# Every second low part of the down weights by an adding transfer instead of a VectorE subtraction

## The chip, the cores and the metric

The kernel runs on one core of a Trainium2 chip. The metric is the time of one execution on the device in microseconds (us). TensorE (PE) multiplies matrices, VectorE (DVE), ScalarE (ACT) and GpSimd (POOL) work elementwise, and SyncE (SP) issues transfers, which run on 16 DMA engines. Here POOL has so far had only small jobs.

## The reference, cut to what matters

One encoder layer over 256 tokens of width 2048: a SwiGLU feed-forward layer of width 5632, attention, a second such feed-forward layer, and a gated embedding, each between two RMS norms. The part that the change touches is the product with `w_down` of both feed-forward layers.

```python
def _swiglu(u, w_gate, w_up, w_down):
    return (jax.nn.silu(u @ w_gate) * (u @ w_up)) @ w_down

for i in range(DEPTH):
    f = _swiglu(_rmsnorm(h, ffn1_pre_g[i]), ffn1_w_gate[i], ffn1_w_up[i], ffn1_w_down[i])
    h = h + 0.5 * _rmsnorm(f, ffn1_post_g[i])
    m = _mixer(_rmsnorm(h, mix_pre_g[i]), w_qkv[i], na_rpb[i], out_g[i], w_o[i])
    h = h + _rmsnorm(m, mix_post_g[i])
    f = _swiglu(_rmsnorm(h, ffn2_pre_g[i]), ffn2_w_gate[i], ffn2_w_up[i], ffn2_w_down[i])
    h = h + 0.5 * _rmsnorm(f, ffn2_post_g[i])
```

All inputs are float32.

## The kernel before, in words

**Split products.** A float32 value does not fit TensorE's fast format fp32r, so each operand is split into a high part, rounded to fp32r, and a low part, the rest. A product is then three matmuls: high by high, low by high, high by low (lines 114, 115, 116). The activations' split lies ready in SBUF (`xh`, `xl`); the weights are split as they arrive.

**load_pairs** (line 62) does that. A transfer on SP's queue (line 69) brings four blocks of 128 weight rows by 512 columns, 1 MB, into a tile `raw`, of which there are three. Blocks are split in pairs: ScalarE writes the high parts of two blocks into a tile `wh`, VectorE the low parts into a tile `wl`; there are seven of each. Where the rows carry a gain `g` (gate, up, q, k, v and others) lines 79 and 80 do it block by block. Where they carry none, line 74 copies 128 x 1024 elements with rounding, and line 75 subtracts: `wl = raw - wh`. Only the down weights and the small `w_ple_proj` come without a gain.

**product** (line 89) walks through the rows of a product in steps of up to eight blocks. For each step it calls `load_pairs`, then multiplies: for the first 128 tokens all eight blocks, three matmuls each, then for the second 128 tokens the same eight blocks again. A step of eight is 48 matmuls, two `raw` tiles (here called A and B) and four pairs, P0 and P1 from A, P2 and P3 from B.

**The order of the work.** A scheduler keeps each engine's instructions close to the program's order; an engine executes its own in order and waits at semaphores for the others. `wh` and `wl` tiles are taken in turn, so pair number n waits until PE has read pair n - 7 for the second tokens. That means that P0, P1 and P2 of a step can be split a whole step ahead, while P3 waits for P0 of the step just before it: PE reads that for the last time early in the second half of that step. A `raw` tile comes free for SP's next load when its last reader is done.

**swiglu** (line 220) works in three groups of 4, 4 and 3 column blocks of 512 (`FF_GROUPS`): gate and up for each block of the group, then the down product of the group's 16, 16 or 12 row blocks into each of four column blocks of the output (line 276). 16 rows are two steps of eight; 12 rows are a step of four and one of eight. A group of 16 rows has so 8 steps of eight in a row, and there are four such groups in the kernel (two per layer): 32 steps. The two groups of 12 rows add 8 steps of eight, each between steps of four.

Of the kernel before, what the change touches and what calls it, by code (L numbers as in the profile page):

```python
# [10 lines left out]
AF = mybir.ActivationFunctionType  # L11
ALU = mybir.AluOpType
# [21 lines left out]
def encoder_layer(ctx: ExitStack, tc: tile.TileContext, a: dict, out: bass.AP):  # L34
# [6 lines left out]
    nc = tc.nc  # L41
# [19 lines left out]
    def load_pairs(w, r0, nk, c0, g):  # L61


        pairs = []
        for k0 in range(0, nk, 4):
            n = min(4, nk - k0)
            raw = wpool.tile([P, 4, NB], F32, name="raw", bufs=3)
            rows_ = w[r0 + k0 * P : r0 + (k0 + n) * P, c0 : c0 + NB]
            raw_loads.append(nc.sync.dma_start(raw[:, :n], rows_.rearrange("(k p) n -> p k n", p=P)))
            for j in range(0, n, 2):  # L70
                wh = wpool.tile([P, 2, NB], F32R, name="wh", bufs=7)
                wl = wpool.tile([P, 2, NB], F32R, name="wl", bufs=7)
                if g is None:
                    nc.scalar.copy(wh, raw[:, j : j + 2])  # L74
                    nc.vector.tensor_tensor(wl, raw[:, j : j + 2], wh.bitcast(F32), op=ALU.subtract)  # L75
                else:
                    for i in range(min(2, n - j)):
                        k = r0 // P + k0 + j + i
                        nc.scalar.activation(wh[:, i], raw[:, j + i], AF.Copy, scale=g[:, k : k + 1])  # L79
                        nc.vector.scalar_tensor_tensor(  # L80
                            wl[:, i], raw[:, j + i], g[:, k : k + 1], wh[:, i].bitcast(F32),
                            op0=ALU.mult, op1=ALU.subtract,
                        )
                pairs.append((wh, wl))
        return pairs
# [3 lines left out]
    def product(  # L89
# [11 lines left out]
        for n in steps or [nk % SUPER] * (nk % SUPER > 0) + [SUPER] * (nk // SUPER):  # L101
            if ahead is not None:
                ahead(s0)
            pairs = load_pairs(w, r0 + s0 * P, n, c0, g)
            for t in range(NT):
                tok = slice(t * P, (t + 1) * P)
                for k in range(n):
                    if mid is not None and t == NT - 1 and s0 + n == nk and k == n - MID:
                        mid()
                    wh, wl = pairs[k // 2]  # L110
                    xh, xl = lhs[s0 + k]
                    lead = first and s0 + k == 0
                    tail = last and s0 + k == nk - 1
                    nc.tensor.matmul(acc[t], xh[:, tok], wh[:, k % 2], start=lead, stop=False)  # L114
                    nc.tensor.matmul(acc[t], xl[:, tok], wh[:, k % 2], start=False, stop=False)  # L115
                    nc.tensor.matmul(acc[t], xh[:, tok], wl[:, k % 2], start=False, stop=tail)  # L116
            s0 += n
            if jobs:
                for job in later:
                    job()  # L120
                later.clear()
# [173 lines left out]
    with ExitStack() as att:  # L295
# [18 lines left out]
        for t in range(NT):  # L314
            for h0 in range(0, n_h, 2):
                raw = attn.tile([P, 2, S], F32, name="na_raw", tag="pr", bufs=2)
# [292 lines left out]
```

## Time and profile before

| | |
|---|---|
| median of the runs | 1991.86 us (1991.73 to 1991.98) |
| the profiled execution's own time | 1990.87 us |
| its span in the trace | 1988.8 us |
| PE busy | 1969.9 us |
| DVE, ACT busy | 1155.9 us, 1050.2 us |
| POOL busy | 25.4 us, 47 instructions |
| moved by DMA | 377.02 MB, mean 190 GB/s |

The profile is of one execution. A row of its groups names the line, the engine, the operation and the tiles; then stand the count, the busy time in us, the mean of one in ns, and the idle time of that engine just before, with what ended it. A matmul's duration (389 ns) is longer than the distance between two of them, since they are pipelined: distances are read from start to start.

### The profile page before, as it was taken

Reading aid. Unit: us, or ns where it says so; the run is one execution under the profiler, and the core shown is the slowest. Engines: PE = TensorE matmul, PEld = TensorE weight load, DVE = VectorE, ACT = ScalarE, POOL = GpSimd, SP = SyncE. Lnnn points to the kernel's source line nnn. Section 1 sums busy time; section 2 is a strip of 40 time slices with the busy share of each in tenths; the row PEclk is TensorE's granted clock in tenths of the full one; section 3 lists DMA queues with packets and bytes.
Section 4 is the critical chain, followed back from the end, with each engine's and each line's share of the span. In section 5 each row is a group of like instructions: output and inputs, shape, how many; then the busy total and the mean of one; then the engine's idle time right before and its main releaser. Section 6 shows DMA issues by size and latency. Waiting matters only on the chain.

```text
span 1988.8 us, 23482 instructions
## 1 busy us (share of the span) xinstructions
PE 1969.9 (99%) x8936; PEld 1629.7 (82%) x8936; DVE 1155.9 (58%) x1659; ACT 1050.2 (53%) x1613; POOL 25.4 (1%) x47
## 2 busy tenths in 40 slices
PE   8999999999999999999999999999999999999998
PEld 7888888888888877888888888888888888888886
DVE  5755455655465666566565575654465545565764
ACT  7645455544455455655556564544454534454663
POOL 0000000000000000000000000000000000000000
PEclk9999999999999999999999999999999999999999
DMA  8755555555555557364554555555555555555562
GB/s 302 242 192 187 194 193 189 190 191 188 194 198 183 197 183 224 134 201 138 170 170 168 187 192 200 179 203 175 206 181 200 179 201 184 197 183 203 172 213 102
DMA packets 194561, 377.02 MB, mean 190 GB/s; under 512 B 10768, under 2 KB 13968, under 8 KB 194192
## 3 DMA queue, kind: packets, MB, share of 16 engines
q1 hardware_dynamic: 194448, 375.52, 55.1%
q8 instruction: 70, 1.15, 0.2%
q14 instruction: 43, 0.35, 0.0%
HBM read 373.40 MB, written 2.10 MB: 189 GB/s over the span
## 4 chain that ended last, share of the span: by engine, by line
PE 96%; DMA 1%; DVE 1%; ACT 1%; issue 0%; POOL 0%; SPq 0%; DVEq 0%; POOLq 0%; ACTq 0%
PE down L116 8%; PE down L114 8%; PE down L115 8%; PE up L116 8%; PE up L114 8%; PE up L115 8%; PE gate L116 8%; PE gate L115 8%; PE gate L114 8%; PE tr L150 2%; PE q L116 1%; PE q L115 1%; PE q L114 1%; PE pg L116 1%; PE pg L114 1%; PE k L116 1%
## 5 line engine op out<-in xcount | busy, mean ns | idle before, releaser
L79 ACT ACTIVATE wh<-raw,row_g 128x512 fp32r<-128x512 f32 x1024 | 686.7, 717 | 456.0 <-PE up L115 184.2
L80 DVE SCALAR_TENSOR_TENSOR wl<-raw,row_g,wh 128x512 fp32r<-128x512 f32 x1024 | 708.6, 749 | 335.9 <-ACT wh L79 335.8
L75 DVE TENSOR_TENSOR wl<-raw,wh 128x1024 fp32r<-128x1024 f32 x180 | 220.0, 1224 | 167.5 <-ACT wh L74 153.1
L74 ACT CAST wh<-raw 128x1024 fp32r<-128x1024 f32 x180 | 189.8, 1055 | 213.1 <-PE down L115 168.7
L114 PE MATMUL gate<-wh,u_h 128*128 128x512 f32 x704 | 276.5, 393 | 6.0 <-ACT wh L79 6.0
L116 PE MATMUL gate<-wl,u_h 128*128 128x512 f32 x704 | 275.2, 391 | 0.0
L115 PE MATMUL gate<-wh,u_l 128*128 128x512 f32 x704 | 275.1, 391 | 0.0
L114 PE MATMUL down<-wh,hid_h 128*128 128x512 f32 x704 | 274.5, 390 | 0.0
L116 PE MATMUL down<-wl,hid_h 128*128 128x512 f32 x704 | 274.1, 389 | 0.0
L116 PE MATMUL up<-wl,u_h 128*128 128x512 f32 x704 | 274.0, 389 | 0.1
L114 PE MATMUL up<-wh,u_h 128*128 128x512 f32 x704 | 274.0, 389 | 0.0
L115 PE MATMUL down<-wh,hid_l 128*128 128x512 f32 x704 | 273.9, 389 | 0.0
L115 PE MATMUL up<-wh,u_l 128*128 128x512 f32 x704 | 273.9, 389 | 0.0
L114 PEld LDWEIGHTS gate<-wh,u_h 128*128 128x128 f32 x704 | 132.9, 189 | 32.9 <-ACT wh L79 6.0
L116 PEld LDWEIGHTS gate<-wl,u_h 128*128 128x128 f32 x704 | 132.7, 188 | 27.9 <-DVE wl L80 0.3
L116 PEld LDWEIGHTS up<-wl,u_h 128*128 128x128 f32 x704 | 132.1, 188 | 28.2 <-DVE wl L80 0.5
L115 PEld LDWEIGHTS gate<-wh,u_l 128*128 128x128 f32 x704 | 132.8, 189 | 27.0
L114 PEld LDWEIGHTS up<-wh,u_h 128*128 128x128 f32 x704 | 132.1, 188 | 27.5 <-ACT wh L79 0.3
L115 PEld LDWEIGHTS up<-wh,u_l 128*128 128x128 f32 x704 | 132.1, 188 | 27.4
L115 PEld LDWEIGHTS down<-wh,hid_l 128*128 128x128 f32 x704 | 132.2, 188 | 27.4
L116 PEld LDWEIGHTS down<-wl,hid_h 128*128 128x128 f32 x704 | 132.1, 188 | 27.4
L114 PEld LDWEIGHTS down<-wh,hid_h 128*128 128x128 f32 x704 | 132.2, 188 | 27.0
(122 smaller groups left out, 1813.6 us busy)
## 6 DMA issues: line engine op xcount, KB each, us to landing
raw<-in_ffn_w_up SPq DMA_DIRECT2D x88, 1024.0 KB, 5.1
raw<-in_ffn_w_down SPq DMA_DIRECT2D x88, 1024.0 KB, 5.0
raw<-in_ffn_w_gate SPq DMA_DIRECT2D x84, 1024.0 KB, 5.1
raw<-in_w_qkv SPq DMA_DIRECT2D x48, 1024.0 KB, 5.1
raw<-in_w_o SPq DMA_DIRECT2D x16, 1024.0 KB, 5.0
raw<-in_w_ple_gate SPq DMA_DIRECT2D x16, 1024.0 KB, 5.0
raw<-in_ffn_w_gate SPq DMA_DIRECT2D x7, 512.0 KB, 4.4
xb<-in_xT SPq DMA_DIRECT2D x8, 256.0 KB, 3.2
```

The lines of the kernel that those rows point to most:

```text
L74: nc.scalar.copy(wh, raw[:, j : j + 2])
L75: nc.vector.tensor_tensor(wl, raw[:, j : j + 2], wh.bitcast(F32), op=ALU.subtract)
L79: nc.scalar.activation(wh[:, i], raw[:, j + i], AF.Copy, scale=g[:, k : k + 1])
L80: nc.vector.scalar_tensor_tensor(wl[:, i], raw[:, j + i], g[:, k : k + 1], wh[:, i].bitcast(F32), op0=ALU.mult, op1=ALU.subtract,)
L114: nc.tensor.matmul(acc[t], xh[:, tok], wh[:, k % 2], start=lead, stop=False)
L115: nc.tensor.matmul(acc[t], xl[:, tok], wh[:, k % 2], start=False, stop=False)
L116: nc.tensor.matmul(acc[t], xh[:, tok], wl[:, k % 2], start=False, stop=tail)
L150: nc.tensor.transpose(tr[:, k], x[:, k * P : (k + 1) * P], ident)
```

## The change

In a step of more than four blocks without a gain, the second pair of each `raw` tile (`j` = 2: P1 and P3) no longer goes through VectorE. ScalarE writes `wh` as before, then writes the negative of the rounded weight into `wl` (line 76 of the changed kernel), and a transfer on GpSimd's queue adds the raw weights to it in SBUF (line 77): `wl = -high + raw`. The first pair of each tile (`j` = 0), steps of four, and `w_ple_proj` are made as before. Lines behind the edit move down by 5, so line 74 of before is 79, 75 is 80, 116 is 121.

```diff
             for j in range(0, n, 2):
                 wh = wpool.tile([P, 2, NB], F32R, name="wh", bufs=7)
                 wl = wpool.tile([P, 2, NB], F32R, name="wl", bufs=7)
-                if g is None:
+                if g is None and j and nk > 4:
+
+                    nc.scalar.copy(wh, raw[:, j : j + 2])
+                    nc.scalar.activation(wl, raw[:, j : j + 2], AF.Copy, scale=-1.0)
+                    nc.gpsimd.dma_start(wl, raw[:, j : j + 2], accum_op=ALU.add)
+                elif g is None:
                     nc.scalar.copy(wh, raw[:, j : j + 2])
                     nc.vector.tensor_tensor(wl, raw[:, j : j + 2], wh.bitcast(F32), op=ALU.subtract)
```

How the instructions stand on ScalarE in the first feed-forward layer, first group, second column block (`down_1667` before and `down_1671` after are its accumulator for the first tokens, the number plus one that for the second). Before:

```order
L264 COPY f<-down_1514 128x512
L74 CAST wh<-raw 128x1024 x4
L264 COPY f<-down_1667 128x512
L74 CAST wh<-raw 128x1024 x4
L264 COPY f<-down_1668 128x512
```

With the change:

```order
L269 COPY f<-down_1514 128x512
L79 CAST wh<-raw 128x1024
L75 CAST wh<-raw 128x1024
L76 ACTIVATE wl<-raw 128x1024
L79 CAST wh<-raw 128x1024
L75 CAST wh<-raw 128x1024
L76 ACTIVATE wl<-raw 128x1024
L79 CAST wh<-raw 128x1024
L269 COPY f<-down_1671 128x512
L75 CAST wh<-raw 128x1024
L76 ACTIVATE wl<-raw 128x1024
L79 CAST wh<-raw 128x1024
```

Each step has gone from four to six conversions on ScalarE; the two new ones stand right behind the high parts of P1 and P3.

GpSimd between the factors of the first feed-forward layer's input norm and those of its output norm, before:

```order
L138 TENSOR_SCALAR m<-m 128x1
L139 TENSOR_TENSOR r<-m,mhalf 128x1
L138 TENSOR_SCALAR m<-m 128x1
L139 TENSOR_TENSOR r<-m,mhalf 128x1
```

With the change:

```order
L143 TENSOR_SCALAR m<-m 128x1
L144 TENSOR_TENSOR r<-m,mhalf 128x1
L77 DMA wl<-raw 128x1024 x40
L143 TENSOR_SCALAR m<-m 128x1
L144 TENSOR_TENSOR r<-m,mhalf 128x1
```

All 40 transfers of a layer stand alone on that queue; nothing else is between them. The second layer has 40 more.

TensorE in the first step of that column block, first tokens, from the second matmul of the third block on (`DMASW` is the semaphore of a transfer issued by GpSimd):

```order
L120 MATMUL down_1671<-wh,hid_l 128x512
L121 MATMUL down_1671<-wl,hid_h 128x512 [waits DMASW4_49]
L119 MATMUL down_1671<-wh,hid_h 128x512
L120 MATMUL down_1671<-wh,hid_l 128x512
L121 MATMUL down_1671<-wl,hid_h 128x512
```

TensorE's order is the same as before, but the third matmul of the third block (P1) and of the seventh (P3) now wait for the adding transfer in place of VectorE.

SP's loads of the down weights wait for it too, since it reads `raw`. Before:

```order
L69 DMA raw<-in_ffn_w_down 128x4x512 [waits DMAHW0_49,DVE_49]
```

With the change:

```order
L69 DMA raw<-in_ffn_w_down 128x4x512 [waits DMASW0_49,DMAHW3_49,DVE_49,Activation_49]
```

The place is a load into a `raw` tile whose last reader was VectorE and now is the adding transfer.

## The prediction

> **What bounds the kernel now.** I read the page first: engines, granted clock, chain, queues.
>
> ```profile
> PE 1969.9 (99%) x8936; PEld 1629.7 (82%) x8936; DVE 1155.9 (58%) x1659; ACT 1050.2 (53%) x1613; POOL 25.4 (1%) x47
> PE   8999999999999999999999999999999999999998
> PEclk9999999999999999999999999999999999999999
> PE 96%; DMA 1%; DVE 1%; ACT 1%; issue 0%; POOL 0%; SPq 0%; DVEq 0%; POOLq 0%; ACTq 0%
> q1 hardware_dynamic: 194448, 375.52, 55.1%
> ```
>
> TensorE is busy for 1969.9 of 1988.8 us at a full granted clock, and 96% of the chain of waits is TensorE. The change leaves its matmuls alone, so at most the 19 us in which it idles could be won, and its slices show those at the start and the end, where no down weight is split. What counts is whether TensorE begins to wait. The last row gives the resource that the change draws on: weight loads fill 55.1% of the 16 DMA engines.
>
> Next the down stage itself, by windows: two steps of eight (208.26 to 230.02 us), and about one step of four and one of eight in the 12-row group.
>
> ```profile
> core 0: us, PE busy (x) PEld busy (x) DVE busy (x) ACT busy (x) POOL busy (x), PEclk, DMA share, GB/s
> 208.26:230.02 21.76, 21.76 (x97) 18.02 (x96) 9.80 (x9) 9.51 (x10) 0.00 (x0) 1.00 0.55 193
> 675.20:691.50 16.30, 16.30 (x78) 13.58 (x77) 11.02 (x12) 8.29 (x12) 0.00 (x0) 1.00 0.50 171
> ```
>
> TensorE fills the window. VectorE and ScalarE work for less than half of the two steps. DMA is busy for 0.55 x 21.76 = 12.0 us, 6.0 us per step of 10.88 us; a step has two loads, so one load of 1 MB takes all engines for 3.0 us.
>
> **What comes off and on the compute engines.**
>
> ```profile
> L79 ACT ACTIVATE wh<-raw,row_g 128x512 fp32r<-128x512 f32 x1024 | 686.7, 717 | 456.0 <-PE up L115 184.2
> L75 DVE TENSOR_TENSOR wl<-raw,wh 128x1024 fp32r<-128x1024 f32 x180 | 220.0, 1224 | 167.5 <-ACT wh L74 153.1
> L74 ACT CAST wh<-raw 128x1024 fp32r<-128x1024 f32 x180 | 189.8, 1055 | 213.1 <-PE down L115 168.7
> L116 PE MATMUL down<-wl,hid_h 128*128 128x512 f32 x704 | 274.1, 389 | 0.0
> ```
>
> Each of the 40 steps of eight loses two subtractions: 80 x 1.224 = 98 us off VectorE. It is off the chain: the subtractions themselves wait for ScalarE, and the matmuls that read them show 0.0 us of idle time ahead. Worth: 0. ScalarE gets 80 negating copies. The trace has none; the nearest row is line 74, the same tile shape and types, 1.055 us, so 84 us. Its bounds are line 79's 0.717 us for half the size with a scale, and twice that, 1.43 us: 57 to 115 us. They fit: 9.51 + 4 x 1.055 = 13.7 of 21.76 us per two steps. Without that cover they would cost 84 us. GpSimd gets 80 issues, with 25.4 us of work in the whole kernel; nothing of it stands between them, so what they cost there is latency, counted next.
>
> **The time that P3's transfer has.** P1 and the other pairs can be made a step ahead; P3 waits for a buffer that comes free in the step before. Timeline rows, the first three TensorE, then ScalarE and VectorE:
>
> ```profile
> 214.84 0.39 PE L115 MATMUL down<-wh,hid_l 128*128 128x512 f32 x1
> 219.14 0.39 PE L116 MATMUL down<-wl,hid_h 128*128 128x512 f32 x1
> 223.90 0.39 PE L116 MATMUL down<-wl,hid_h 128*128 128x512 f32 x1
> ...
> 215.26 1.05 ACT L74 CAST wh<-raw 128x1024 fp32r<-128x1024 f32 x1 [5.27 <-PE down L115]
> 216.62 1.06 ACT L74 CAST wh<-raw 128x1024 fp32r<-128x1024 f32 x1 [0.30 <-PE down L115]
> ...
> 216.35 5.30 DVE L75 TENSOR_TENSOR wl<-raw,wh 128x1024 fp32r<-128x1024 f32 x4 [5.57 <-ACT wh L74]
> ```
>
> At 214.84 PE reads the high part of P0's second block for the last time, and ScalarE starts on P3 of the next step at 215.26. A step ends with the matmul at 219.14; from there to 223.90 are 21 matmuls, 0.227 us each, 48 of them 10.88 us. The one at 223.90 is the seventh block's third, the first to read P3's `wl`. VectorE has it ready at about 217.6, 6.3 us early. Now ScalarE writes high part and negative by 215.26 + 2 x 1.055 = 217.4, and the transfer has 223.9 - 217.4 = **6.5 us** from issue to landing. Each us above is a stall of TensorE in each of 32 steps. P1's negative is the fifth conversion of that round, ready at 215.26 + 5 x 1.055 and short waits, about 221, and first read in the third block of the step after next, 219.37 + 10.88 + 8 x 0.227 = 232.1: 11 us. In the 12-row groups P3 takes P2's buffer, free some 2.9 us later, and a step of four, 5.44 us, lies between: 9 us.
>
> Behind a late transfer SP waits too: `raw` comes free only when it has landed, and SP's queue is in order.
>
> ```profile
> SPq L69 <- DVE wl L75: 442.1, 92, 8.8
> raw<-in_ffn_w_down SPq DMA_DIRECT2D x88, 1024.0 KB, 5.0
> raw<-in_ffn_w_gate SPq DMA_DIRECT2D x7, 512.0 KB, 4.4
> raw<-in_w_ple_proj SPq DMA_DIRECT2D x4, 512.0 KB, 3.8
> ```
>
> SP waits up to 8.8 us for that reader as it is, 442.1 / 92 = 4.8 us on average, then loads for 5.0 us. So the loads have slack, and one may come some us later without ScalarE going short.
>
> **What one adding transfer costs.** No transfer within SBUF and none on GpSimd's queue is in this trace, so I bound it by loads. A load of 512 KB lands after 3.8 to 4.4 us, one of 1 MB after 5.0, of which 3.0 are moving; about 2.0 are fixed. Low end: 512 KB pass once, 1.5 us of all engines, landing in 3.8. Middle: the engines must fetch the old `wl` as well as `raw`, so 1 MB is read: 3.0 us, landing in 5.0 alone. High end: four passes (two reads, the sum, the write) one after the other, 6.0 us. I take the middle, since adding cannot be done without the second read, and writing can run beside reading, as it does in the loads.
>
> The Trainium skill says the same of reduction by DMA on the page "Collectives: The Full Stack", section "The bandwidth ceiling: the fold count and why AG ≠ RS ≠ AR": the add itself is not what makes it slower, the two source reads are, and they halve the rate. Its page "DMA: Bandwidth & Descriptors", section "Anatomy of one DMA — SWDGE (gpsimd) path", gives 2.0 us plus bytes / 436e3 for a transfer from GpSimd, an estimate of 3.2 us for 512 KB; by that P3 would have 3.3 us to spare and the change would cost nothing. No row here shows either.
>
> **The sum.** Demand on the DMA engines per step of eight: 6.0 + 2 x 3.0 = 12.0 us in a step of 10.88 us. So they become the bound: 1.1 us per step. The other view is latency: 5.0 us alone; when a load is in flight beside it all the time, sharing the engines by half, 3.0 more, 8.0 us, a stall of 1.5. With the engines full, the second is nearer. I take 1.3 us: 32 x 1.3 = **42 us**. The 12-row groups: three loads, 9.0, plus 6.0 is 15.0 in 16.3 us, 0. ScalarE, VectorE, GpSimd: 0. Against the profiled execution: 1990.9 + 42 = 2033; the median is 1 us above that, so **2034 us**, 2.1% slower. Its own range is 0.6 to 2.1 us per step, 2011 to 2059.
>
> **Rivals.**
>
> *Hidden.* The second read costs the engines little, or SBUF answers faster than the memory the loads read. With up to 2.4 us a transfer the demand is 10.8 us, and landing stays below 6.5. For it: 3.8 us for a plain 512 KB leave 2.7 us of room. Against it: there is nearly no reserve, with two users on the same engines. Time: 1992, not slower.
>
> *Slow adding.* The passes are not overlapped. Three of them, 4.5 us per transfer: 6.0 + 9.0 = 15.0 per step, 4.1 over, 132 us; in the 12-row groups 9.0 + 9.0 = 18.0 in 16.3, 8 x 1.7 = 14 us: 2138. Four: 7.1 x 32 + 4.7 x 8 = 265 us, 2257. Nothing in this profile speaks for or against.
>
> *GpSimd is slow to issue.* If writing out the transfer takes 4 us more than SP's 2.0 fixed, it lands after 9.0 alone, and P3 stalls TensorE for 2.5 us while the engines still have idle time: 32 x 2.5 = 80 us, 2072. The row that bears on it is thin:
>
> ```profile
> L425 POOL TENSOR_TENSOR ro<-sso,mhalf 128x4 f32<-128x4 f32 x8 | 8.5, 1059 | 304.4 <-DVE sso L423 304.4
> L69 SPq DMA_DIRECT2D raw<-in_ffn_w_down x88: 367/368/368, 162.2 to 1844.7; - x88
> ```
>
> GpSimd takes 1.06 us for four elements per partition, where SP issues a whole load in 0.37.
>
> *It brings something.* VectorE's 98 us would have to stand on the chain; TensorE's waits on it there sum to nothing in the page's groups. 1985 would be a third of TensorE's 19 idle us.
>
> **Chances.** Forecast 0.36, hidden 0.28, slow adding 0.24, slow issue 0.11, a gain 0.01. A measurement tells about 2%, here 40 us, from no change: 2032. The forecast lies on that line; I give 0.17 of it to the near side. Same: 0.28 + 0.17 + 0.01 = 0.46. Slower: 0.19 + 0.24 + 0.11 = 0.54 less 0.01 for the cheapest of the slow issues: 0.53. Faster: 0.01. The range starts at the hidden case, 1989, and ends behind the three passes, 2140; left out are some 0.1 above (four passes) and little below.
>
> **What would show it.** In the window of the 16-row groups: DMA share of 0.9 or more, steps of about 12.2 us, TensorE waiting for the transfer `wl<-raw` at line 121 once per step, in the seventh block; landing of these transfers 7 to 8 us; ScalarE's new group of 80 near 1.05 us each; no idle TensorE in the 12-row groups. Wrong if the DMA share stays near 0.8 (the second read is cheap) or if TensorE idles while the DMA engines do too (issue or fixed latency).

## The result

The changed kernel takes 2009.55 us (2009.52 to 2009.58, two runs) where the kernel before took 1991.86: 17.7 us more, ratio 1.0093, 95% interval 1.0074 to 1.0111. The forecast was 42 us more. So it is slower, by less than the 2% that a small measurement tells from no change, and by 0.42 of the predicted amount. The profiled execution took 2009.58 us, its span is 2007.8 us, 19.0 us longer than before. One execution of a version below, the one with the 12-row groups alone, took 11468.67 us; it is left out of that version's numbers.

### The profile page after: what moved, and what is told of

It reads as the page before. It is cut to its first block, busy times and chain, and to the rows that moved or that the text cites. A ratio compares the mean times of both kernels' runs of the same rounds, so it can differ in the third digit from the quotient of the medians.

```text
span 2007.8 us, 23858 instructions
## 1 busy us (share of the span) xinstructions
PE 1976.0 (98%) x8936; PEld 1631.1 (81%) x8936; DVE 1060.9 (53%) x1579; ACT 1115.9 (56%) x1693; POOL 94.8 (5%) x127
## 4 chain that ended last, share of the span: by engine, by line
PE 79%; issue 12%; DMA 6%; DVE 1%; ACT 1%; POOL 1%; POOLq 0%; SPq 0%; DVEq 0%; ACTq 0%
PE gate L121 7%; PE gate L120 7%; PE gate L119 7%; PE up L121 7%; PE up L119 7%; PE up L120 7%; PE down L121 4%; PE down L120 4%; PE down L119 4%; DMA wl<-raw 2%; DMA raw<-in_ffn_w_down 2%; PE tr L155 2%; PE q L119 1%; PE q L121 1%; PE q L120 1%
## 5 line engine op out<-in xcount | busy, mean ns | idle before, releaser
L80 DVE TENSOR_TENSOR wl<-raw,wh 128x1024 fp32r<-128x1024 f32 x100 | 122.5, 1225 | 286.8 <-ACT wh L79 279.2
L75 ACT CAST wh<-raw 128x1024 fp32r<-128x1024 f32 x80 | 83.9, 1049 | 135.7 <-PE down L120 102.2
```

## The profile after

First the page of the changed kernel, in the order in which the prediction read that of before: engines, the new queue, the chain, the new DMA issues.

```profile
PE 1976.0 (98%) x8936; PEld 1631.1 (81%) x8936; DVE 1060.9 (53%) x1579; ACT 1115.9 (56%) x1693; POOL 94.8 (5%) x127
q0 software_dynamic: 11520, 41.95, 11.0%
PE 79%; issue 12%; DMA 6%; DVE 1%; ACT 1%; POOL 1%; POOLq 0%; SPq 0%; DVEq 0%; ACTq 0%
wl<-raw POOLq DMA_DIRECT2D x80, 512.0 KB, 4.9
```

VectorE gave up 95 us and ScalarE took on 66. The chain, 96% TensorE before, now runs for 6% over transfers and for 12% over "issue", time for which the profile names no cause. Nearly all of that lies in the 16-row groups, so there the chain is known in part only. The new queue takes 11.0% of the 16 DMA engines' time in the span: 0.110 x 2007.8 / 80 = **2.76 us of all engines per transfer**, and the median landing is 4.9 us after the issue.

The windows of the same stretches as before, the 16-row group made longer to four steps of eight, and a stretch of about the same work in the 12-row group:

```profile
core 0: us, PE busy (x) PEld busy (x) DVE busy (x) ACT busy (x) POOL busy (x), PEclk, DMA share, GB/s
208.26:251.78 43.52, 43.52 (x193) 36.05 (x193) 8.94 (x8) 24.68 (x28) 6.95 (x8) 1.00 1.01 278
675.00:691.50 16.50, 16.50 (x79) 13.74 (x78) 7.46 (x9) 8.67 (x12) 1.74 (x2) 1.00 0.81 247
```

The DMA engines are full (1.01) through four steps. **TensorE is full in the very same 43.52 us**, at exactly 10.88 us per step: full engines alone do not show in the time. In the 12-row group there is room, as forecast.

The places where TensorE does wait, in its timeline (start, duration, then in brackets the idle time and what ended it), and its waits in sum (us in total, times, longest); of the three waits for `hid_l` one is shown. The last row is the transfer's time from issue to landing:

```profile
258.45 0.50 PE L121 MATMUL down<-wl,hid_h 128*128 128x512 f32 x1 [1.71 <-DMA wl<-raw]
468.63 0.51 PE L120 MATMUL down<-wh,hid_l 128*128 128x512 f32 x1 [0.88 <-DVE hid_l L158]
525.11 0.50 PE L121 MATMUL down<-wl,hid_h 128*128 128x512 f32 x1 [0.19 <-DMA wl<-raw]
1382.02 0.56 PE L121 MATMUL down<-wl,hid_h 128*128 128x512 f32 x1 [2.21 <-DMA wl<-raw]
...
1661.68 0.50 PE L121 MATMUL down<-wl,hid_h 128*128 128x512 f32 x1 [1.20 <-DMA wl<-raw]
1673.47 0.50 PE L121 MATMUL down<-wl,hid_h 128*128 128x512 f32 x1 [0.61 <-DMA wl<-raw]
1686.32 0.50 PE L121 MATMUL down<-wl,hid_h 128*128 128x512 f32 x1 [1.67 <-DMA wl<-raw]
1893.07 0.63 PE L155 MATMUL tr<-ident,h 128*128 128x128 f32 x4 [2.50 <-DVE h L215]
```

```profile
PE down L121 <- DMA wl<-raw: 7.6, 6, 2.2
PE tr L155 <- DVE h L215: 3.5, 2, 2.5
PE tr L155 <- issue: 2.5, 2, 2.0
PE down L120 <- DVE hid_l L158: 2.0, 3, 0.9
DMA to landing us min/median/max: 4.4/4.9/8.7
```

Six waits for the transfer, not 32. Counted in matmuls from the start of their group, they stand in its fifth (once), sixth (once), seventh (three times) and eighth step (once), never in the first four, and each at the third matmul of the seventh block, where P3's `wl` is first read. The transfers behind the first and the longest of them stand in the chain (start and time to landing):

```profile
250.24 8.16 DMA wl<-raw
1373.30 8.67 DMA wl<-raw
```

Their landing less the 6.5 us that the prediction gives P3 is 1.66 and 2.17 us, and TensorE waits 1.71 and 2.21. For all six it is so: they land after 6.64 to 8.67 us, and each wait is what lies above 6.5, to 0.05 us. Of the 80 transfers only two others need more than 6.5 us, and nobody waits for those. Beside the six waits there are waits that the forecast did not have: for `hid_l` early in a group, and for `tr`, the transposes of the next stage, behind a 12-row group (2.7 us in sum before, 6.0 now). There is a third loss, in the granted clock, the third column from the end of these windows:

```profile
1382.00:1386.00 4.00, 3.98 (x11) 3.13 (x12) 0.00 (x0) 0.03 (x1) 0.00 (x0) 0.57 0.73 220
1386.00:1390.00 4.00, 4.00 (x19) 3.30 (x18) 0.91 (x1) 3.96 (x5) 0.86 (x1) 1.00 0.93 343
1893.00:1897.00 4.00, 3.93 (x16) 3.29 (x17) 3.98 (x7) 3.07 (x7) 0.00 (x0) 0.66 0.96 326
1897.00:1901.00 4.00, 4.00 (x17) 3.24 (x17) 2.55 (x5) 3.59 (x9) 0.77 (x2) 0.91 0.14 49
```

After the waits of 2.21 and 2.50 us the clock is down: (0.43 + 0.34 + 0.09) x 4 us = 3.4 us of work lost, an estimate. Together 7.6 + 2.0 + (6.0 - 2.7) + 3.4 = 16.3 of the 19.0 us. Measured from start to start, less the usual 0.227 us, the nine stalls in the down products come to 11.1 us instead of 9.6, so some 1.2 us have no row.

How much later the same instruction runs than before, read from both timelines at the border of each stage:

| behind | us later | lost in it |
|---|---|---|
| start of the first down group | -0.7 | |
| layer 1, first and second 16-row group | 2.2, 4.0 | 2.9, 1.8 |
| layer 1, 12-row group and its norm | 5.4 | 1.4 |
| layer 2, first and second 16-row group | 9.7, 15.0 | 4.3, 5.3 |
| layer 2, 12-row group and its norm | 18.5 | 3.5 |

## The experiments

**Theory:** the transfers fill the DMA engines in the 16-row groups; what is over demand comes to TensorE as a late `wl`. **First rival:** the engines are not what limits, and P3's transfer is late because its buffer comes free late. Later a second one came up: a transfer holds its `raw` tile longer, SP's next load stands behind it, and ScalarE, in order, comes late with other work. All edits are to the changed kernel; ratios are to the kernel before, on the same chip, with 95% intervals.

### One transfer per step: P1 alone and P3 alone

```diff
-                if g is None and j and nk > 4:
+                if g is None and j and nk > 4 and k0 == 0:
```

(P1 alone; P3 alone has `k0 == 4`.)

> Only P1, the second pair of each first raw tile, is made by the transfer (40 in place of 80); P3 is VectorE's again. Full engines: demand per step of eight is 6.0 us of loads and one transfer of about 2.6, 8.6 of 10.88 us, so no backlog: 1992 to 1995, DMA share in the 16-row groups near 0.8. Late P3 (its landing against the 6.5 us it has): P3 no longer comes by transfer, 1992 to 1993. ScalarE's extra copies as the cause: half of the loss stays, about 2001.

> Only P3, the pair with the short allowance, is made by the transfer (40 in place of 80). Full engines: the same demand as with P1 alone, 8.6 of 10.88 us, 1992 to 1995, landing below 5.5 us. Late P3: every tight transfer is still there, so most of the 17.7 us stays, 2003 to 2010. ScalarE's extra copies: about 2001.

P1 alone: 1992.10 us, 1.0006 (0.9996 to 1.0015). P3 alone: 1991.24 us, 1.0004 (0.9994 to 1.0013). Neither costs anything that can be measured. P3 alone, its window and its landing:

```profile
208.26:251.78 43.52, 43.52 (x194) 36.04 (x193) 13.99 (x13) 21.94 (x25) 3.44 (x4) 1.00 0.81 241
DMA to landing us min/median/max: 4.4/4.5/5.7
```

With the engines at 0.81 the transfer lands after 4.5 us, at worst 5.7, inside the 6.5 us that P3 has. The late buffer alone is ruled out as the cause; what is left needs both transfers of a step.

### The same number on the first pairs

```diff
-                if g is None and j and nk > 4:
+                if g is None and not j and nk > 4:
```

> The first pair of each raw tile (P0 and P2) is made by the transfer and the second by VectorE: the same 80 transfers, but no pair that has to wait for a buffer of the step before. Full engines: the demand of 11.2 us in 10.88 is the same, loads fall behind and starve ScalarE at the end of each group: 2003 to 2012, DMA share 0.97 or more. Late P3: P0 and P2 have over 10 us, so 1992 to 1995.

1998.43 us, 1.0041 (1.0026 to 1.0056): 8.0 us, under half of the change's loss and between both expectations. The engines are nearly as full as in the change (0.98 against 1.01), and the transfers land later:

```profile
208.26:251.78 43.52, 42.94 (x189) 35.23 (x189) 9.80 (x8) 23.43 (x27) 6.57 (x8) 1.00 0.98 269
DMA to landing us min/median/max: 4.7/6.5/10.7
```

Its three waits for the transfer (0.58, 1.64 and 0.78 us) stand at 244.87, 257.70 and 269.68 us, in the last three steps of the first group, and none in the other three. Read against before as in the table above, its four 16-row groups lose 4.3 us where the change loses 14.3; most of the rest comes behind the second layer's 12-row group. So equal demand does not give an equal loss. Here 39 of the 80 transfers need more than 6.5 us, and only three are waited for, since P0 and P2 have more time. With P3 alone on engines that have room, none needs more than 5.7. So it takes both, full engines and the pair with little time.

### Twice as many

```diff
-                if g is None and j and nk > 4:
+                if g is None and nk > 4:
```

> All four pairs of a step of eight are made by the transfer (160). Full engines: 6.0 + 4 x 2.6 = 16.4 us per step, 5.5 over, 32 steps 177 us, and in the 12-row groups 9.0 + 10.4 = 19.4 in 16.3, 25 us, less some 12 us that the buffers take up: 2150 to 2200, DMA share 1.0. Late P3: the P3s of 40 steps wait as with the change, behind a few more transfers, 2010 to 2040.

2174.16 us, 1.0933 (1.0902 to 1.0964): 183.7 us, as the full engines foretold.

```profile
q0 software_dynamic: 23040, 83.90, 19.9%
208.26:251.78 43.52, 39.13 (x146) 30.55 (x146) 1.29 (x2) 26.05 (x30) 10.41 (x12) 0.88 1.04 253
PE down L121 <- DMA wl<-raw: 98.0, 57, 7.7
PE down L119 <- ACT hid_h L157: 19.4, 4, 7.5
```

The loss comes to TensorE as waits, most of them these, and as a lower clock: 0.972 in the mean of the trace against 0.999 before, an estimated 59 us of 2173.

A transfer takes 0.199 x 2173.2 / 160 = 2.70 us, nearly the same as in the change. The demand is 6.0 + 4 x 2.7 = 16.8 us per step of eight, 5.9 over, and by the prediction's reckoning 9.0 + 10.8 = 19.8 in the 16.3 us of a 12-row column block, 3.5 over: 32 x 5.9 + 8 x 3.5 = 217 us. The 33 us that are not lost are 5.5 us for each of the six groups. That is an estimate of how far the tiles in SBUF let the transfers fall behind before TensorE notices. In the change the excess is 6.0 + 2 x 2.76 - 10.88 = 0.6 us per step, 5 us over the eight steps of a group: about as much as the tiles can take. By this sum alone the change would lose next to nothing in these groups. The waits come nevertheless, since single transfers land beyond P3's 6.5 us before the excess of a whole group has gathered.

### What the adding costs: a plain copy, and no transfer

```diff
-                    nc.gpsimd.dma_start(wl, raw[:, j : j + 2], accum_op=ALU.add)
+                    nc.gpsimd.dma_start(wl, raw[:, j : j + 2])
```

It leaves the sum out, `wl` gets the raw weight; all transfers, copies and waits stay. The other puts VectorE's subtraction in the place of the transfer, behind the negating copy, which is then not used:

```diff
-                    nc.gpsimd.dma_start(wl, raw[:, j : j + 2], accum_op=ALU.add)
+                    nc.vector.tensor_tensor(wl, raw[:, j : j + 2], wh.bitcast(F32), op=ALU.subtract)
```

> The transfer copies the raw weights over the negative in place of adding to it: one read instead of two. Leaves out the sum, so the low parts of these pairs are wrong. If the second read is what makes the transfer dear (2.7 us of the engines): some 1.5 to 1.8 us, demand 9.0 to 9.6 of 10.88 us, landing near 4 us, time 1990 to 1994. If it is the way through GpSimd's queue or within SBUF, whatever is read: 2.7 us again, 2005 to 2010.

> ScalarE writes the negative as in the change, but VectorE then makes the low part as before; no transfer. ScalarE's 80 extra copies alone. If they cost nothing, as the sum has it: 1990 to 1993. If ScalarE's order costs (its queue is where gate, transposes and squares stand too): 1996 or more.

The plain copy: 1991.97 us, 1.0006 (0.9997 to 1.0016). Without a transfer: 1991.21 us, 1.0003 (0.9993 to 1.0012). So the negating copies on ScalarE and 80 transfers with their waits cost nothing that shows; it is the adding. Whether its second read or the sum itself takes the engines' time, no run here parts. One thing more differs: GpSimd issues a plain copy in 0.54 us, an adding transfer in 0.87. The plain copy's rows:

```profile
q0 software_dynamic: 11520, 41.95, 5.9%
208.26:251.78 43.52, 43.52 (x194) 36.04 (x192) 9.81 (x8) 25.30 (x29) 4.30 (x8) 1.00 0.83 289
DMA to landing us min/median/max: 2.8/3.5/5.8
```

The queue's bytes are the same as in the change, its time is 0.059 x 1988.4 / 80 = 1.47 us per transfer against 2.76: 1.9 times. The Trainium skill, page "Collectives: The Full Stack", section "The bandwidth ceiling: the fold count and why AG ≠ RS ≠ AR", says that two source reads halve the rate of a reduction by DMA; the factor of 1.9 in this trace agrees, within one core's SBUF, though it doesn't show that the read is the reason.

### Two of the four column blocks: the first two, and the middle two

```diff
-                if g is None and j and nk > 4:
+                if g is None and j and nk > 4 and c0 < 2 * NB:
```

(The middle two have `c0 in (NB, 2 * NB)`: as many transfers, as dense, but none in the first steps of a group nor in its last.)

> Both transfers per step, but only in the first two of the four column blocks of each group (40 transfers, four steps in a row at the full demand). If a backlog builds up and the buffers take up the first part of it: under 3 us, 1990 to 1994. If each step at full demand costs TensorE the same: half the loss, 1998 to 2001.

> Both transfers per step, 40 in all, in the second and third of the four column blocks of each group; as many and as dense as in the run with the first two blocks, which lost 0.2%. If what that run lost was the entry (the transposed hidden part's casts stand on ScalarE behind a load that a transfer holds up): 1990 to 1992. If it is the density of four steps at full demand: 1994 to 1996 again.

The first two blocks: 1994.76 us, 1.0020 (1.0010 to 1.0030). The middle two: 1991.61 us, 1.0007 (0.9998 to 1.0016). The wait that the first adds to those of before, then the window and the added wait of the second:

```profile
PE down L120 <- DVE hid_l L158: 2.5, 3, 0.9
```

```profile
208.26:251.78 43.52, 43.52 (x193) 36.00 (x192) 12.66 (x11) 23.93 (x27) 5.17 (x6) 1.00 0.98 278
PE down L121 <- DMA wl<-raw: 2.0, 2, 1.6
```

Neither loses what half of 17.7 us would be; the first two lie a little above what was expected of a backlog that the buffers take up. Four steps in a row with full engines (0.98) cost 1.5 us by the medians, which the interval doesn't tell from nothing. Their excess of 2.4 us lies below the estimate of what the tiles take up, yet the profiled execution has two waits, in the second and the fourth of these steps of two groups, for a P3 that landed after 6.86 and 8.01 us. And the first two blocks, with the same excess, have another wait, at the entry of the group, that the middle two have not.

### Half the bytes in as many transfers

```diff
-                    nc.gpsimd.dma_start(wl, raw[:, j : j + 2], accum_op=ALU.add)
+                    nc.gpsimd.dma_start(wl[:, 0], raw[:, j], accum_op=ALU.add)
```

It leaves the second half of each tile as the negative high part.

> The same 80 transfers at the same places, each adding the raw weights of the first block of its pair only, 256 KB in place of 512. Leaves out the sum for the second block, so its low parts are wrong. Full engines: 1.4 us of the engines each, demand 6.0 + 2.8 = 8.8 of 10.88 us, no backlog, 1990 to 1994, landing under 4.5 us. If the number of transfers, their issue on GpSimd and the waits on their semaphores are what costs: the loss stays, 2004 to 2010.

1997.43 us, 1.0037 (1.0025 to 1.0050): 7.2 us, between the two expectations; both missed it. In the profile:

```profile
208.26:251.78 43.52, 43.52 (x194) 36.04 (x193) 9.81 (x8) 25.41 (x29) 6.95 (x8) 1.00 0.82 240
PE down L120 <- DVE hid_l L158: 2.4, 4, 0.9
PE down L121 <- DMA wl<-raw: 0.2, 1, 0.2
```

The engines have room, the transfer is waited for once, for 0.2 us, and still time is lost: the wait for `hid_l`. These rows account for some 2.6 of the 5.2 us by which the profiled execution (1995.38 us) is longer than the median of before (1990.18); the rest of the 7.2 us is not explained. But they brought up the second cause, which the changed kernel's rows at the entry of its second group show, ScalarE and then the chain:

```profile
462.83 1.05 ACT L79 CAST wh<-raw 128x1024 fp32r<-128x1024 f32 x1 [1.31 <-DMA raw<-in_ffn_w_down]
...
466.62 1.06 ACT L157 CAST hid_h<-tr 128x512 fp32r<-128x512 f32 x2
```

```profile
450.93 4.45 DMA wl<-raw
455.52 7.21 DMA raw<-in_ffn_w_down
```

By the last two rows a transfer lands at 455.38, the load behind it on its `raw` tile goes out at 455.52 and lands at 462.73, and ScalarE, which has waited for it since 461.5, splits at 462.83. Behind that in ScalarE's order, at 466.62, stands the rounding of the last hidden columns, for which TensorE waits at 468.63. With half the bytes the same split waits 0.61 us for its load; in the plain copy, which is issued 0.33 us faster and lands after 3.5 us in place of 3.8, it does not wait (at 460.92). Their engine time is nearly the same (1.47 against 1.52 us a transfer), so at this entry a few tenths of a microsecond in the landing decide, and not how full the engines are.

### The 12-row groups left out, alone, and without their last block

```diff
-                if g is None and j and nk > 4:
+                if g is None and j and nk > 4 and r0 < 8 * NB:
```

(Alone: `r0 >= 8 * NB`; without the last column block: that and `c0 < 3 * NB`.)

> As the change, but the 12-row groups are made by VectorE again (64 transfers). If the 12-row groups cost nothing, as the sum had it: the loss stays, 2007 to 2010. If their share is what the comparison of events in the two traces gives, some 4 to 5 us: 2002 to 2005.

> The change in the 12-row groups only (16 transfers, two in each of 8 steps of eight, with a step of four between). Demand 9.0 + 2 x 2.7 = 14.4 of 16.3 us. If these groups cost nothing when no backlog comes in from a 16-row group: 1990 to 1993. If the late first loads behind the last transfer of each group cost what the two traces' comparison gives: 1994 to 1996.

> As the run with the 12-row groups only, but the last column block of each is VectorE's again (12 transfers). If those groups cost time because the next stage's first load waits behind their last transfer, and ScalarE's queue then holds the norm's squares behind that load: 1990 to 1992. If every transfer there costs some: three quarters of the loss of that run stay, 1994 to 1995.

Left out: 2006.53 us, 1.0078 (1.0063 to 1.0093), between its two expectations; the interval overlaps the change's, so it doesn't show what the 12-row groups cost, but it gives the 16-row groups alone, 15.9 us. The 12-row groups alone, 16 transfers: 1995.47 us in the median of six, 1.0026 (1.0014 to 1.0037). Without the last block, 12 transfers: 1991.58 us, 1.0005 (0.9995 to 1.0014). The 12-row groups do cost something, 5.3 us where the forecast had 0, and all of it hangs on four transfers, two for the last column block of each group. The rows with the 12-row groups alone:

```profile
PE tr L155 <- DVE h L215: 3.3, 2, 2.3
DMA to landing us min/median/max: 4.4/4.7/5.0
```

The transfers land in 5.0 us at most; no engine is full, and no down product waits. The granted clock falls behind both seams as well, at 737 and 1880 us, some 1.7 us of work each. What is late is the next stage's load. The changed kernel's end of the last group shows it: GpSimd's issue, SP with its waits from 1855 to 1885 us, ScalarE, VectorE:

```profile
1874.12 0.86 POOL L77 DMA_DIRECT2D wl<-raw  x1 [12.99 <-ACT wl L76]
```

```profile
1866.29 0.46 SPq L134 DMA_DIRECT2D g_post<-in_ple_post_g  x1
1878.62 3.68 SPq L69 DMA_DIRECT2D raw<-in_w_ple_proj  x3
```

```profile
SPq L69 <- DMA wl<-raw: 28.0, 4, 11.8
```

```profile
1884.49 1.05 ACT L79 CAST wh<-raw 128x1024 fp32r<-128x1024 f32 x1 [6.25 <-DMA raw<-in_w_ple_proj]
```

```profile
1885.57 2.53 DVE L80 TENSOR_TENSOR wl<-raw,wh 128x1024 fp32r<-128x1024 f32 x2 [6.10 <-ACT wh L79]
1888.02 0.68 DVE L271 TENSOR_TENSOR f<-f,down 128x512 f32<-128x512 f32 x1
```

Before, the same sum waited for TensorE alone:

```profile
1871.10 0.69 DVE L266 TENSOR_TENSOR f<-f,down 128x512 f32<-128x512 f32 x1 [3.31 <-PE down L116]
```

With the change, the transfer issued at 1874.12 reads the `raw` tile that SP's next load wants; it needs 4.4 us, and the load goes out at 1878.62. SP has sent nothing for 12 us by then, ScalarE stands 6.25 us before the split of the embedding's weight, VectorE behind ScalarE, and behind VectorE's two subtractions stands the last sum of `f`, from which the norm, `h` and the transposes at 1893.07 follow. This was followed in the second layer only; at the first layer's seam the profile names no cause for the wait. No version was faster than the kernel before.

## Why the prediction was half right

*TensorE is the bound, VectorE's 98 us are worth nothing.* Right: 95 us came off VectorE and the kernel did not gain; with its subtractions back (no transfer) the time is that of before.

*ScalarE's 80 negating copies at 1.055 us, free.* Right in price (1.055 us measured; ScalarE's busy time rises by 66 us and not by 84, since copies back to back overlap by some 0.1 us) and in effect: the kernel without a transfer has them all and is not slower.

*GpSimd's issue.* Right to leave at nothing: 69.4 us for 80, 0.87 us each, and with 40 of them (P1 or P3 alone) nothing is lost. The rival of a slow issue, landing after 9.0 us, is out: with room on the engines the transfer lands after 4.4 to 4.5.

*An adding transfer takes 3.0 us of all engines, for the second read.* Right in kind, a tenth too high: 2.76 in the change, 2.70 with twice as many, 1.47 without the add; that the read is the reason stays argued. The 3.2 us to landing that the prediction quotes beside its sum are near the plain copy's 3.5 and too low for the adding transfer's 4.4 to 4.9. Slow adding is out; of the rival "hidden" it is only true that one transfer per step is hidden.

*The DMA engines become the bound in the 16-row groups.* Right as far as they are full (share 1.01) and doubling the transfers costs 184 us. But a full engine isn't yet a bound on the time: TensorE is full beside it for four steps, and a step takes 10.88 us, not the 12.2 that were to be seen.

*32 steps x 1.3 us = 42 us.* **Wrong: this is the term that was mis-sized.** The excess is 0.5 to 0.6 us per step, not 1.1 to 1.5, since a price of 2.7 instead of 3.0 halves what is left above 10.88. And neither the excess nor the late landing is paid in each step: four full steps cost nothing that can be measured (the middle blocks, 1.0007). The way to the wait was right to the tenth, landing less 6.5 us at the seventh block, but the landing was to be 7 to 8 us in each step and is 4.9 in the median, above 6.5 for the P3 of six steps out of 32, none of them among the first four of a group. All that the 16-row groups lose is 15.9 us (the run without the 12-row groups; 14.3 in the table), 0.5 us per step where 1.3 stood. By the trace, late transfers have 7.6 us of waits and half of the lowered clock, 1.7 us: 9 us where 42 stood.

*The 12-row groups: 0.* Wrong. The engines do have room there (0.81), and that was the only thing that the term asked. The last block's transfers keep `raw` from the next stage: 5.3 us alone, gone without that block.

*Loads have slack, ScalarE does not go short.* Wrong. ScalarE waits for a load of down weights 29 times, 39.5 us in sum ahead of its line 79; before, no such wait shows ahead of the same casts. In the middle of a group that costs TensorE nothing that shows, since pairs lie ready; at the entry and at the end other work stands behind ScalarE's split in its order. The prediction named the late load and stopped there, without asking what stands behind the instruction that waits for it.

The clock's loss of 3.4 us was in no term. The 16-row groups alone (15.9 us) and the 12-row groups alone (5.3) add to 1.04% against the change's 0.93% (0.74 to 1.11), so the parts add up within their intervals. How the loss in the 16-row groups splits between late landing (the waits for `wl`) and late `raw` (those for `hid_l`) was read from one trace and not measured apart: more `raw` or `wl` tiles, which would have parted them, weren't tried. Nor is it shown why those six transfers land late and the other P3s do not. That the second layer loses twice as much as the first in the same work also stays open.

## What to carry to other kernels

An excess of demand over a shared resource need not be paid in each step: add it up over a run of such steps and ask what the buffers hold and which consumer has the least time, or a small error in the price will be multiplied by the count. Here the sum over a group less the buffers would have given about nothing and the product per step gave 42 us, where 15.9 were measured. A wait itself is landing less the time that the tile's reader allows; how many transfers land beyond that is what has to be known. Where an operation gets a later last reader of a tile, follow the tile on: the next load into it, the in-order engine that waits for that load, and what stands behind on that engine, above all at the first and last step of a stage. Doing the suspected work in half and in twice the places tells quickly whether a cost is linear; here half cost 0, all 18 and twice 184 us.

## What the hardware showed

A short stall can lower TensorE's clock: after idle times of 2.21 us (in the down product) and 2.50 us (behind the last group) the granted clock was 0.57 and 0.66 over the next 4 us and 1.00 and 0.91 over the 4 us behind those, some 1.7 us of work lost each time. The length alone doesn't decide it. In the changed kernel the clock stayed at 1.00 after waits of 1.71 us (258.45) and 2.03 us (741.63); with the 12-row groups alone it was 0.57 after one of 1.70 us (736.14), in the last row:

```profile
258.40:262.40 4.00, 3.95 (x17) 3.28 (x18) 0.00 (x0) 1.56 (x2) 0.00 (x0) 1.00 0.70 204
741.60:745.60 4.00, 3.89 (x21) 3.21 (x22) 4.00 (x7) 3.02 (x6) 0.00 (x0) 1.00 0.00 0
737.00:741.00 4.00, 4.00 (x14) 3.24 (x14) 2.57 (x5) 2.31 (x5) 0.00 (x0) 0.57 0.00 0
```

The Trainium skill, page "TensorE: Matmul & The Clock Gate", section "HAM oscillation — how this bites in real kernels", speaks of idle gaps above some 3.4 us; here less was enough, and the measurement decides. So the wait of 2.50 us was worth about 4.2.
